# A hybrid encoder on one core: half of a shift vector summed on TensorE, small loads on another queue, the first loads reordered

## The chip, the core and the metric

The kernel runs on one core of a Trainium2 chip. The metric is the device time of one execution in microseconds (us). Engines are named as the profile names them: PE is TensorE (PEld its weight loads), DVE is VectorE, ACT is ScalarE, POOL is GpSimd, SP is SyncE, which issues nearly all DMA loads.

## The reference

Two layers work on 256 tokens of 1024 channels in fp32. Each layer is a feed-forward sub-layer (FFN), a token mixer (pooling in layer 0, latent attention in layer 1) and a second FFN. Every sub-layer is modulated by vectors that come from a condition `c`:

```python
sc = jax.nn.silu(c)
mod = (sc @ ada_w[i] + ada_b[i]).reshape(B, N_MOD, D_MODEL)[:, :, None, :]   # shift, scale, gate x 3

def modulated_sublayer(x, mod, g_pre, g_post, fn, weight):
    shift, scale, gate = mod[:, 0], mod[:, 1], mod[:, 2]
    h = rmsnorm(x, g_pre) * (1.0 + scale) + shift
    y = rmsnorm(fn(h), g_post)
    return x + weight * (1.0 + gate) * y

def swiglu(h, w_in, w_out):
    gate, up = jnp.split(h @ w_in, 2, axis=-1)
    return (jax.nn.silu(gate) * up) @ w_out
```

`sc` has 1024 entries and each layer's `ada_w` is 1024 x 9216, so a shift or a scale is a vector-matrix product of 1024 x 1024. The first FFN can't start before its shift and scale are known. The change touches only this opening.

## The kernel before

**Tiling.** The 256 tokens are two tiles of 128 (t = 0 and 1). A weight is loaded by SP in pieces of 128 x 2048 fp32 (1 MiB) into one of four raw buffers. It is then split for matmuls in a faster fp32 form: ACT casts it to a high part (`wi10H`, L263) and DVE subtracts to get a low part (`wi10L`, L271); a product is three matmuls (L98 to L100). The FFN goes through its 2816 columns in eleven chunks of 256. Pieces of the input weight are called by chunk and half of the 1024 rows: `wi10` is chunk 1, first half. Chunks 0 and 2 multiply their first half in plain fp32 (`task_in_whole`, matmuls at L794), without a split.

**Shift and scale.** A vector (m = 0 the shift, 1 the scale) is made in halves of 512 columns, each from two 1 MiB pieces (`adah`). DVE adds up eight terms, each a [128 x 512] weight times one column of `sc` (L350, then seven of L352), and PE sums over the partitions with the accumulated tile as weights and a column of ones as the moving operand (`ps_mod`, L361); DVE adds the bias (`mod`, L374). In this opening these are finished one after another as the code below calls them.

**The opening.** x is turned to [channel, token] tiles by PE (`ps_h`, L562, a half of 512 channels at a time), scaled and shifted into `hs` (ACT at L576 for one tile, DVE at L582 for the other), then split into `hTH` and `hTL`. `head_first` runs the first-half matmuls of chunks 0, 1 and 2 for both tiles, and between them steps a generator, `first_halves`, which brings in the second halves of shift and scale and the second halves of h; then the rest. Small matmuls on the identity (`warm`, L108) fill waits of PE.

**What sets the order.** Nothing is scheduled: each engine runs its instructions in the order in which the code issues them. Loads go out in the order of the list `first`, one list entry a task; a task's load is issued when one of the four raw buffers is free, that is, when DVE has finished the task four such pieces ahead (`Bulk.advance`). A DMA also takes one of eight completion lanes in turn, and waits until the lane's last DMA has landed.

Of the kernel before, what the change touches and what calls it, by code (L numbers as in the profile page):

```python
# [17 lines left out]
P = 128  # L18
D = 1024
# [20 lines left out]
def kernel(  # L40
# [71 lines left out]


    c_col = cpool.tile([P, KD], F32, name="c_col")
    nc.sync.dma_start(c_col, c_in.rearrange("o (p k) -> p (o k)", k=KD))
    xt = [rowp.tile([P, D], F32, tag=f"x{t}", name=f"x{t}", bufs=1) for t in range(NT)]

    def load_x(t):
        nc.sync.dma_start(xt[t], x_in[0, t * P : (t + 1) * P, :])
# [7 lines left out]
    ones = ones_r.bitcast(F32)  # L127
    mhalf = cpool.tile([P, 1], F32, name="mhalf")
    nc.vector.memset(mhalf, -0.5)
    sc = cpool.tile([P, KD], F32, name="sc")  # L130
    nc.scalar.activation(sc, c_col, AF.Silu)


    cols = cpool.tile([P, 96 + 144 + 3], F32, name="cols")
# [1 line left out]
    C_Q = 96 + 144  # L136
    C_KV = C_Q + 2

    def load_columns(parts, base):
        rows = rowp.tile([P, 512], F32, tag="bc", name="rows", bufs=4)[:, :P]  # L140
        n = 0
        for ap in parts:
            r = ap.shape[0]
            nc.sync.dma_start(rows[n : n + r, :], ap)
# [12 lines left out]
    def load_columns_late():  # L157
        return load_columns(
# [157 lines left out]
    def ada_half(layer, m, hf, accs, pieces=(1, 1)):  # L316

        st = {}
        wv = ada_w[layer].rearrange("(p k) n -> p k n", k=KD)
        c0 = m * D + hf * 512  # L320

        def load(q):
            def go():
                raw = raw_tile(f"adah{m}{hf}{q}")
                rv = raw.rearrange("p (k n) -> p k n", k=4)
                for k in range(0, 4, 4 // pieces[q]):
                    ks = slice(k, k + 4 // pieces[q])
# [1001 lines left out]


    accs = {}
    first = ada_half(0, 0, 0, accs) + ada_half(0, 1, 0, accs, (1, 2))
    with_load = lambda t, f: (t[0], lambda: (t[1](), f()), *t[2:])
    first[1] = with_load(first[1], lambda: load_x(0))
    first[2] = with_load(first[2], lambda: load_x(1))
    h01, h11 = ada_half(0, 0, 1, accs), ada_half(0, 1, 1, accs, (1, 2))
    first += [f0.task_in_whole(0, 0), h01[0], f0.task_in(1, 0), h01[1], *h11, f0.task_in_whole(2, 0)]
    ss1 = shift_scale(0, 1)
    first += [f0.task_in(0, 1), ss1[0], f0.task_in(1, 1), ss1[1], f0.task_in(2, 1), f0.task_out(0)]
    first += [ss1[2], f0.task_out(1), ss1[3], f0.task_in(3, 0), f0.task_in(3, 1)]  # L1340
# [50 lines left out]
        )  # L1391


    bulk.until(("adah", 0, 0, 1))
    turn_g()
    turn_b()
    bulk.finish_pe()
    s20 = first_rstd(0)
    xr0 = pre_xr(0, s20)
    bulk.until(("adah", 1, 0, 0))  # L1400
    bulk.finish()
    s21 = first_rstd(1)
    xr1 = pre_xr(1, s21)
    hT = [new_hT(0), new_hT(1)]
    turned = [turn_half(0, 0, xr0)]
    warm(6, "acc11", 1)
    turned += [turn_half(1, 0, xr1, psum.tile([P, 512], F32, tag="acc10", name="ps_h10", bufs=1))]
    warm(4, "acc11", 1)
    bulk.until(("adah", 1, 0, 1))
    bulk.finish()  # L1410
    parts = [mod_half(t, 0, ps, hT[t], 0, 0, t == 1) for t, ps in enumerate(turned)]

    def first_halves():
        bulk.until(("adah", 0, 1, 0))
# [12 lines left out]
        f0.high_in(0, 1)  # L1427
        bulk.finish()
        late += [turn_half(1, 1, xr1)]
        late = [mod_half(t, 1, ps, hT[t], 0, 0, t == 0) for t, ps in enumerate(late)]  # L1430
# [2 lines left out]
        for _, low, _ in late:  # L1433
            low()
        yield
        yield

    f0.head_first(hT, [p[2] for p in parts], first_halves())
    turn_late = load_columns_late()
    f0.unit(3, 0, hT[0])  # L1440
    f0.unit(3, 1, hT[1])
# [238 lines left out]
```

## Time and profile before

| | us |
|---|---|
| median of three runs (lowest, highest) | 925.95 (924.56, 929.2) |
| the profiled execution | 930.35 |
| its span | 928.6 |
| PE busy in the span | 898.9 |
| DVE busy | 703.9 |
| ACT busy | 437.3 |

The profiled execution is slower than the median by 4.4 us. The span leaves out 1.75 us around it. PE is busy 97% of the span; the forty slices of the page show the first one at 3 tenths for PE and all others but the last at 9. A busy PE need not be at full speed: the page's clock row is at 8 tenths in the second slice and in one near 645 us. The 16 DMA engines move 325 to 373 GB/s in four of the first five slices and 299 in the third.

### The profile page before, as it was taken

To read this page: it belongs to the slowest core of one execution; us is meant where nothing else is said; L and a number is where in the kernel's file an instruction comes from. 1 tells how busy PE (TensorE), PEld (TensorE's weight loads), DVE (VectorE), ACT (ScalarE), POOL (GpSimd) and SP (SyncE) were. 2 spreads that over 40 slices of the span, in tenths; PEclk is the share of its full clock that TensorE was granted. 3 is DMA by queue.
4 is the path that set the end of the run, shared out by engine and by line. 5 is a ranking of instruction groups with operands and counts; after the bars stand their busy time and mean duration, and the time that the engine had idled before them with its cause. 6 is when DMAs were issued, how large, how long until landed. Compare 5 with 4: busy or idle time off the path is not lost.

```text
span 928.6 us, 11171 instructions
## 1 busy us (share of the span) xinstructions
PE 898.9 (97%) x4251; PEld 733.0 (79%) x4251; DVE 703.9 (76%) x848; ACT 437.3 (47%) x653; POOL 41.8 (5%) x56
## 2 busy tenths in 40 slices
PE   3999999999999999999999999999999999999997
PEld 3568887887888888888888888888776888888885
DVE  5798888887877898797867987766798765656553
ACT  2255443345645434334742534337698654343421
POOL 0000000000000000000000000001163000000000
PEclk9899999999999999999999999998999999999999
DMA  9989998996357999898469999961143458857601
GB/s 325 368 299 343 360 373 313 351 359 242 137 180 264 378 339 326 297 387 275 137 183 360 324 351 327 344 229 59 46 137 113 160 153 280 293 193 259 227 1 45
DMA packets 135973, 235.28 MB, mean 253 GB/s; under 512 B 5628, under 2 KB 98415, under 8 KB 135664
## 3 DMA queue, kind: packets, MB, share of 16 engines
q1 hardware_dynamic: 135920, 234.58, 72.8%
q8 instruction: 33, 0.54, 0.2%
q14 instruction: 20, 0.16, 0.1%
HBM read 233.51 MB, written 1.05 MB: 253 GB/s over the span
## 4 chain that ended last, share of the span: by engine, by line
PE 88%; DVE 7%; issue 2%; DMA 1%; ACT 1%; POOL 0%; SPq 0%; DVEq 0%; POOLq 0%; ACTq 0%
PE acc L747 25%; PE in L100 16%; PE in L98 16%; PE in L99 16%; PE accm L1319 2%; PE ps_g L724 2%; DVE aacc L352 1%; PE ps_h L562 1%; PE ps_mod L361 1%; PE in L794 1%; DVE nm L1220 1%; DVE ql L1203 1%; DMA wo<-in_ffn_w_out_dram 1%; PE accp L965 1%; DMA adah<-in_ada_w_dram 1%
## 5 line engine op out<-in xcount | busy, mean ns | idle before, releaser
L352 DVE SCALAR_TENSOR_TENSOR aacc<-ada,sc,aacc 128x1024 f32<-128x1024 f32 (+1 forms) x113 | 143.8, 1272 | 9.9 <-DMA ada<-in_ada_w_dram 7.6
L708 ACT ACTIVATE sil<-in 128x256 f32<-128x256 f32 x84 | 32.2, 383 | 247.0 <-PE in L100 242.1
L710 DVE TENSOR_TENSOR g<-in,sil 128x256 f32<-128x256 f32 x84 | 35.2, 419 | 52.0 <-ACT sil L708 51.9
L95 DVE TENSOR_TENSOR gL<-ps_g,gH 128x256 fp32r<-128x256 f32 x88 | 36.6, 416 | 23.6 <-ACT gH L94 23.5
L94 ACT CAST gH<-ps_g 128x256 fp32r<-128x256 f32 x88 | 32.4, 368 | 44.5 <-PE ps_g L724 44.4
L503 POOL TENSOR_TENSOR r<-ms,mhalf 128x1 f32<-128x1 f32 x24 | 13.6, 565 | 840.5 <-DVE ms L501 840.5
L724 PEld LDWEIGHTS ps_g<-ident,g 128*128 128x128 f32 x176 | 24.7, 140 | 11.5
L724 PE MATMUL ps_g<-ident,g 128*128 128x128 f32 x176 | 33.6, 272 | 0.0
L508 ACT ACTIVATE junk<-x 128x512 bf16<-128x512 f32 x24 | 15.1, 631 | 21.1 <-DVE x L535 11.3
L361 PE MATMUL ps_mod<-ones,aacc 128*128 128x1 f32 x96 | 12.9, 262 | 10.9 <-DVE cols L150 9.7
L361 PEld LDWEIGHTS ps_mod<-ones,aacc 128*128 128x128 f32 x96 | 13.2, 213 | 11.9 <-DVE cols L150 10.0
L576 ACT ACTIVATE hs<-ps_h,mod,mod 128x128 f32<-128x128 f32 x48 | 18.0, 456 | 8.6 <-DVE mod L377 5.5
L352 DVE SCALAR_TENSOR_TENSOR aacc<-adah,sc,aacc 128x512 f32<-128x512 f32 x28 | 21.0, 751 | 0.9
L582 DVE TENSOR_SCALAR hs<-ps_h,mod,mod 128x128 f32<-128x128 f32 x48 | 16.4, 403 | 4.9 <-PE ps_h L562 4.6
L535 DVE SCALAR_TENSOR_TENSOR x<-tmp,r,x 128x512 f32<-128x512 f32 x23 | 16.3, 748 | 2.2 <-POOL r L503 1.2
L1238 POOL TENSOR_SCALAR p<-p,rs 128x256 f32<-128x256 f32 x16 | 16.1, 1008 | 26.8 <-ACT p L1228 16.4
L1228 ACT ACTIVATE p<-s,nm 128x256 f32<-128x256 f32 x32 | 15.0, 478 | 4.0 <-DVE nm L1220 2.6
L554 ACT ACTIVATE xr<-x,r 128x512 f32<-128x512 f32 x12 | 8.7, 722 | 17.4 <-POOL r L503 17.4
L593 DVE TENSOR_TENSOR hTL<-hs,hTH 128x512 fp32r<-128x512 f32 x24 | 15.6, 689 | 0.4
L271 DVE TENSOR_TENSOR wo10L<-wo,wo10H 128x2048 fp32r<-128x2048 f32 x4 | 9.2, 2292 | 8.1 <-ACT wo10H L263 8.1
L397 DVE TENSOR_REDUCE mod<-ps_turn 128x4 f32<-128x512 f32 x12 | 8.2, 687 | 8.1 <-PE ps_turn L391 8.1
L562 PE MATMUL ps_h<-ident,xr 128*128 128x128 f32 x96 | 13.7, 283 | 0.5 <-ACT xr L554 0.3
(498 smaller groups left out, 2880.3 us busy)
## 6 DMA issues: line engine op xcount, KB each, us to landing
wi<-in_ffn_w_in_dram SPq DMA_DIRECT2D x176, 512.0 KB, 5.8
ada<-in_ada_w_dram SPq DMA_DIRECT2D x64, 1024.0 KB, 7.1
wo<-in_ffn_w_out_dram SPq DMA_DIRECT2D x44, 1024.0 KB, 6.4
adah<-in_ada_w_dram SPq DMA_DIRECT2D x6, 1024.0 KB, 10.3
mwo<-in_mla_w_o_dram SPq DMA_DIRECT2D x4, 1024.0 KB, 6.1
bc<-in_ada_b_dram SPq DMA_DIRECT2D x12, 256.0 KB, 6.8
bc<-in_norm_g_dram SPq DMA_DIRECT2D x12, 256.0 KB, 7.4
adah<-in_ada_w_dram SPq DMA_DIRECT2D x4, 512.0 KB, 11.7
```

The lines of the kernel that those rows point to most:

```text
L94: nc.scalar.copy(h, src)
L95: nc.vector.tensor_sub(lo, src, h.bitcast(F32))
L98: nc.tensor.matmul(ps, lhsT=lh, rhs=rh, start=first, stop=False)
L99: nc.tensor.matmul(ps, lhsT=lh, rhs=rl, start=False, stop=False)
L100: nc.tensor.matmul(ps, lhsT=ll, rhs=rh, start=False, stop=last)
L352: nc.vector.scalar_tensor_tensor(acc, w, sc[:, k : k + 1], acc, op0=ALU.mult, op1=ALU.add)
L361: nc.tensor.matmul(ps[:, j : j + 1], lhsT=acc[:, (j - j0) * P : (j - j0 + 1) * P], rhs=ones[:, 0:1], start=True, stop=True,)
L562: nc.tensor.transpose(ps[:, j * P : (j + 1) * P], xr[:, kk * P : (kk + 1) * P], ident)
L708: nc.scalar.activation(sil, ps[:, 0:CW], AF.Silu)
L710: nc.vector.tensor_mul(g, ps[:, CW : 2 * CW], sil)
L724: nc.tensor.transpose(ps[:, a * P : (a + 1) * P], g[:, a * P : (a + 1) * P], ident)
L747: nc.tensor.matmul(acc[hf], lhsT=lhs[:, a, :], rhs=rhs[:, a, hf * 512 : (hf + 1) * 512], start=f, stop=l)
```

## The change

The first half of the first shift (layer 0, m = 0, columns 0 to 511) is summed on PE: `ada_half_pe` loads the two 1 MiB pieces in two DMAs each and runs 32 matmuls with a 128 x 128 block of the weight as the stationary operand and a column of `sc` as the moving one; a matmul with zeros opens the accumulation and one closes it. DVE adds only the bias (L390 of the new file). The loads of `c`, of the norm gains and of the biases are issued by ACT instead of SP. In `first`, wi00, wi10 and the second halves of shift and scale change places. xr0 is scaled by ACT alone, x of tile 1 is scaled and turned later, inside `first_halves`, and the ten small `warm` matmuls become four of 512 columns. The second half of the shift is reduced behind chunk 2's first group, that of the scale behind its second.

```diff
-    nc.sync.dma_start(c_col, c_in.rearrange("o (p k) -> p (o k)", k=KD))
+    nc.scalar.dma_start(c_col, c_in.rearrange("o (p k) -> p (o k)", k=KD))
...
+    zeros = cpool.tile([P, 4], F32, name="zeros")
+    nc.vector.memset(zeros, 0.0)
...
-    turn_g = load_columns([norm_g.rearrange("l m (j p) -> (l m j) p", p=P)], 0)
-    turn_b = load_columns([ada_b[0:1, :].rearrange("l (r p) -> (l r) p", p=P)], C_B)
+    turn_g = load_columns([norm_g.rearrange("l m (j p) -> (l m j) p", p=P)], 0, nc.scalar)
+    turn_b = load_columns([ada_b[0:1, :].rearrange("l (r p) -> (l r) p", p=P)], C_B, nc.scalar)
+
+    nc.scalar.activation(sc, c_col, AF.Silu)
...
+    def ada_half_pe(layer, m, pieces):
+        wv = ada_w[layer].rearrange("(p k) n -> p k n", k=KD)
+        c0 = m * D
+        st = {}
+
+        def load(q):
+            def go():
+                raw = raw_tile(f"adah{m}0{q}")
+                rv = raw.rearrange("p (k n) -> p k n", k=4)
+                for k in range(0, 4, 4 // pieces):
+                    ks = slice(k, k + 4 // pieces)
+                    nc.sync.dma_start(rv[:, ks, :], wv[:, 4 * q + ks.start : 4 * q + ks.stop, c0 : c0 + 512])
+                st[q] = rv
+
+            return go
+
+        def compute(q):
+            def go():
+                if q == 0:
+                    st["ps"] = tr_tile(f"ps_sum{m}")
+                    nc.tensor.matmul(st["ps"][:, 0:4], lhsT=ident, rhs=zeros, start=True, stop=False, skip_group_check=True)
+                ps, rv = st["ps"], st.pop(q)
+                for k in range(4):
+                    for j in range(4):
+                        nc.tensor.matmul(
+                            ps[:, j : j + 1],
+                            lhsT=rv[:, k, j * P : (j + 1) * P],
+                            rhs=sc[:, 4 * q + k : 4 * q + k + 1],
+                            start=False,
+                            stop=False,
+                            skip_group_check=True,
+                        )
+                if q == 1:
+                    nc.tensor.matmul(ps[:, 0:4], lhsT=ident, rhs=zeros, start=False, stop=True, skip_group_check=True)
...
+                    bulk.after.append(
+                        lambda: nc.vector.tensor_add(mods[layer, m][:, 0:4], ps[:, 0:4], cols[:, b : b + 4])
+                    )
...
-    first = ada_half(0, 0, 0, accs) + ada_half(0, 1, 0, accs, (1, 2))
+    first = ada_half_pe(0, 0, 2) + ada_half(0, 1, 0, accs, (2, 2))
...
-    first[2] = with_load(first[2], lambda: load_x(1))
+    first[3] = with_load(first[3], lambda: load_x(1))
...
-    first += [f0.task_in_whole(0, 0), h01[0], f0.task_in(1, 0), h01[1], *h11, f0.task_in_whole(2, 0)]
+    first += [f0.task_in_whole(0, 0), f0.task_in(1, 0), *h01, h11[0], f0.task_in_whole(2, 0), h11[1]]
...
     bulk.until(("adah", 1, 0, 0))
+    r0 = rstd(s20, 1.0)
     bulk.finish()
...
-    warm(6, "acc11", 1)
...
-    warm(4, "acc11", 1)
+    scratch = psum.tile([P, 512], F32, tag="acc11", name="warm", bufs=1)
+    for _ in range(4):
+        nc.tensor.matmul(scratch, lhsT=ident, rhs=xt[0][:, 0:512], start=True, stop=True)
     bulk.until(("adah", 1, 0, 1))
+    s21 = first_rstd(1)
     bulk.finish()
-    parts = [mod_half(t, 0, ps, hT[t], 0, 0, t == 1) for t, ps in enumerate(turned)]
+    parts = [mod_half(0, 0, turned[0], hT[0], 0, 0, False)]
+    h_first = [parts[0][2]]
+    xr1 = pre_xr(1, s21)
 
     def first_halves():
-        bulk.until(("adah", 0, 1, 0))
+        ps = turn_half(1, 0, xr1, psum.tile([P, 512], F32, tag="acc10", name="ps_h10", bufs=1))
+        parts.append(mod_half(1, 0, ps, hT[1], 0, 0, True))
+        h_first.append(parts[1][2])
         yield
         for high, low, _ in parts:
             high()
             low()
+        f0.high_in(1, 0)
         bulk.until(("wi", 0, 0, 1, 0))
+        bulk.until(("adah", 0, 1, 0))
         yield
         bulk.until(("adah", 0, 1, 1))
-        bulk.finish()
+        yield
+        bulk.until(("adah", 1, 1, 0))
+        yield
+        bulk.finish_pe()
         late = [turn_half(0, 1, xr0)]
-        yield
-        yield
         bulk.until(("adah", 1, 1, 1))
...
```

PE's queue before, from the first reduction (`ps_mod`) to the first FFN matmuls (`in`); `x4` counts instructions of the same kind in a row:

```order
L361 MATMUL ps_mod_134<-ones,aacc_111 128x1 x4
L562 MATMUL ps_h_176<-ident,xr_149 128x128 x4
L108 MATMUL warm<-ident 128x128 x6
L562 MATMUL ps_h_188<-ident,xr_169 128x128 x4
L108 MATMUL warm<-ident 128x128 x4
L361 MATMUL ps_mod_204<-ones,aacc_152 128x1 x4
L794 MATMUL in_222<-wi_116,hs_212 128x512 x4
L794 MATMUL in_234<-wi_116,hs_217 128x512 x4
```

The same place in the changed kernel, where `ps_sum` is the new sum:

```order
L373 MATMUL ps_sum_122<-zeros,ident 128x4
L377 MATMUL ps_sum_122<-sc,adah_108 128x1 x16
L377 MATMUL ps_sum_122<-sc,adah_111 128x1 x16
L386 MATMUL ps_sum_122<-zeros,ident 128x4
L611 MATMUL ps_h_190<-ident,xr_183 128x128 x4
L1457 MATMUL warm<-x_80,ident 128x512 x4
L410 MATMUL ps_mod_211<-ones,aacc_171 128x1 x4
L843 MATMUL in_231<-wi_140,hs_219 128x512 x4
L611 MATMUL ps_h_236<-ident,xr_228 128x128 x4
L843 MATMUL in_246<-wi_140,hs_241 128x512 x4
```

The sum and the wide `warm` group stand ahead of the scale's reduction (`ps_mod_211`), and tile 1's transposes (`ps_h_236`) now lie between the two tiles' matmuls of chunk 0.

DVE's queue before, from the shift's sum (`aacc_111`) to the scale's (`aacc_152`):

```order
L350 TENSOR_SCALAR aacc_111<-adah_100,sc 128x512
L352 SCALAR_TENSOR_TENSOR aacc_111<-adah_100,sc,aacc_111 128x512 x3
L352 SCALAR_TENSOR_TENSOR aacc_111<-adah_102,sc,aacc_111 128x512 x4
L150 COPY cols<-ps_cols 128x96
L150 COPY cols<-ps_cols 128x72
L501 SCALAR_TENSOR_TENSOR ms<-s_140 128x1
L555 TENSOR_SCALAR xr_149<-x_80,r 128x512
L350 TENSOR_SCALAR aacc_152<-adah_105,sc 128x512
L352 SCALAR_TENSOR_TENSOR aacc_152<-adah_105,sc,aacc_152 128x512 x3
L374 TENSOR_TENSOR mod_139<-ps_mod_134,cols 128x4
```

And in the changed kernel, from the scale's first half to h:

```order
L399 TENSOR_SCALAR aacc_171<-adah_115,sc 128x512
L401 SCALAR_TENSOR_TENSOR aacc_171<-adah_115,sc,aacc_171 128x512 x3
L550 SCALAR_TENSOR_TENSOR ms<-s_166 128x1
L390 TENSOR_TENSOR mod_163<-ps_sum_122,cols 128x4
L401 SCALAR_TENSOR_TENSOR aacc_171<-adah_118,sc,aacc_171 128x512 x4
L423 TENSOR_TENSOR mod_216<-ps_mod_211,cols 128x4
```

The shift's eight steps are gone from DVE; its bias add (`mod_163`), which reads PE's sum, stands ahead of the scale's last four steps.

PE's queue before, from chunk 2's first group (`first_0`) to the second half of chunk 0:

```order
L794 MATMUL first_0_296<-wi_247,hs_212 128x512 x4
L361 MATMUL ps_mod_317<-ones,aacc_152 128x1 x4
L562 MATMUL ps_h_324<-ident,xr_169 128x128 x4
L794 MATMUL first_1_297<-wi_247,hs_217 128x512 x4
L808 MATMUL in_222<-wi01H,hTH_172 128x512 x4
```

And in the changed kernel:

```order
L843 MATMUL first_0_312<-wi_259,hs_219 128x512 x4
L410 MATMUL ps_mod_318<-ones,aacc_265 128x1 x4
L611 MATMUL ps_h_323<-ident,xr_183 128x128 x4
L843 MATMUL first_1_313<-wi_259,hs_241 128x512 x4
L410 MATMUL ps_mod_340<-ones,aacc_171 128x1 x4
L611 MATMUL ps_h_348<-ident,xr_228 128x128 x4
L857 MATMUL in_231<-wi01H,hTH_186 128x512 x4
```

The scale's second reduction (`ps_mod_340`) comes behind chunk 2's second group now, next to the matmuls that need what is made from it.

## Rows read from the trace of the kernel before

**Rows 1.** Two stretches of PE: bounds, length, busy time (instructions), granted clock, DMA share, GB/s.

```profile
0.00:66.00 66.00, 49.11 (x194) 0.95 0.94 330
66.00:928.00 862.00, 849.82 (x4058) 0.99 0.72 248
```

**Rows 2.** Waits of PE from 60 us on: us in total, times, longest.

```profile
PE acc L747 <- DVE g L710: 1.1, 1, 1.1
```

**Rows 3.** Timeline: start, us, engine, line, operation, count, [idle before it, releaser].

```profile
2.11 0.94 SPq L328 DMA_DIRECT2D adah<-in_ada_w_dram  x2
...
7.44 0.48 DVE L350 TENSOR_SCALAR aacc<-adah,sc 128x512 f32<-128x512 f32 x1 [6.07 <-DMA adah<-in_ada_w_dram]
...
11.35 0.63 ACT L508 ACTIVATE junk<-x 128x512 bf16<-128x512 f32 x1 [8.64 <-DMA x<-in_x_dram]
...
13.65 1.78 PEld L361 LDWEIGHTS ps_mod<-ones,aacc 128*128 128x128 f32 x8 [9.99 <-DVE cols L150]
...
15.25 0.83 PEld L562 LDWEIGHTS ps_h<-ident,xr 128*128 128x128 f32 x4
...
16.06 2.68 PEld L108 LDWEIGHTS warm<-ident 128*128 128x128 f32 x12
...
19.30 0.53 PEld L562 LDWEIGHTS ps_h<-ident,xr 128*128 128x128 f32 x4 [0.55 <-ACT xr L554]
...
22.08 0.98 PEld L361 LDWEIGHTS ps_mod<-ones,aacc 128*128 128x128 f32 x8 [1.31 <-DVE aacc L352]
...
23.64 1.50 ACT L576 ACTIVATE hs<-ps_h,mod,mod 128x128 f32<-128x128 f32 x4 [4.39 <-DVE mod L377]
...
24.04 9.99 PE L794 MATMUL in<-wi,hs 128*128 128x512 f32 x16 [0.90 <-DVE hs L582]
...
25.02 0.63 ACT L590 CAST hTH<-hs 128x512 fp32r<-128x512 f32 x1
...
26.85 1.90 ACT L263 CAST wi10H<-wi 128x2048 fp32r<-128x2048 f32 x1 [1.21 <-DMA wi<-in_ffn_w_in_dram]
...
29.29 2.28 DVE L271 TENSOR_TENSOR wi10L<-wi,wi10H 128x2048 fp32r<-128x2048 f32 x1
...
37.70 0.47 DVE L350 TENSOR_SCALAR aacc<-adah,sc 128x512 f32<-128x512 f32 x1
...
38.21 5.48 DVE L352 SCALAR_TENSOR_TENSOR aacc<-adah,sc,aacc 128x512 f32<-128x512 f32 x7
...
40.66 3.59 PE L794 MATMUL first<-wi,hs 128*128 128x512 f32 x8
...
44.09 0.95 PE L361 MATMUL ps_mod<-ones,aacc 128*128 128x1 f32 x8
...
48.94 2.28 DVE L271 TENSOR_TENSOR wi01L<-wi,wi01H 128x2048 fp32r<-128x2048 f32 x1
```

**Rows 4.** Timeline of PE ahead of the attention layer, same columns.

```profile
640.70 1.84 PE L361 MATMUL ps_mod<-ones,aacc 128*128 128x1 f32 x16
642.40 1.07 PE L562 MATMUL ps_h<-ident,xr 128*128 128x128 f32 x8
643.31 2.58 PE L361 MATMUL ps_mod<-ones,aacc 128*128 128x1 f32 x16
```

**Rows 5.** Stretches of PE as in rows 1, where the granted clock falls.

```profile
23.00:24.00 1.00, 0.15 (x2) 0.50 1.09 358
...
644.00:644.50 0.50, 0.50 (x6) 0.72 0.00 0
644.50:645.00 0.50, 0.50 (x4) 0.50 0.00 0
```

**Rows 6.** All engines' busy time in a stretch; last: granted clock, DMA share, GB/s.

```profile
4.00:8.00 4.00, 0.00 (x0) 0.00 (x0) 0.53 (x2) 0.00 (x0) 0.00 (x0) 1.00 1.02 385
```

**Rows 7.** Timeline of PE's weight loads, chunk 0's first matmuls, columns as in rows 3.

```profile
28.47 0.34 PEld L794 LDWEIGHTS in<-wi,hs 128*128 128x128 f32 x1 [0.52 <-issue]
...
30.44 0.19 PEld L794 LDWEIGHTS in<-wi,hs 128*128 128x128 f32 x1 [0.24 <-issue]
```

More of the change, by code (lines that the diff above doesn't have):

```diff
@@ L137, with load_columns @@
     C_KV = C_Q + 2
-    def load_columns(parts, base):
+    def load_columns(parts, base, queue=nc.sync):
         rows = rowp.tile([P, 512], F32, tag="bc", name="rows", bufs=4)[:, :P]
@@ L143, in load_columns @@
             r = ap.shape[0]
-            nc.sync.dma_start(rows[n : n + r, :], ap)
+            queue.dma_start(rows[n : n + r, :], ap)
             n += r
@@ L346, in ada_half @@
         return [(("adah", m, hf, q), load(q), None, compute(q)) for q in range(2)]
+    def ada_half_pe(layer, m, pieces):
[29 more added lines that the diff above has]
+                    nc.tensor.matmul(ps[:, 0:4], lhsT=ident, rhs=zeros, start=False, stop=True, skip_group_check=True)
+                    mods[layer, m] = cpool.tile([P, KD], F32, name=f"mod{layer}{m}")
+                    b = C_B + layer * 72 + m * KD
+                    bulk.after.append(
+                        lambda: nc.vector.tensor_add(mods[layer, m][:, 0:4], ps[:, 0:4], cols[:, b : b + 4])
+                    )
+            return go
+        return [(("adah", m, 0, q), load(q), None, compute(q)) for q in range(2)]
     def ada_step(acc, w, k):
@@ L1391, in ffn_tail @@
         )
-    bulk.until(("adah", 0, 0, 1))
     turn_g()
     turn_b()
-    bulk.finish_pe()
+    bulk.until(("adah", 0, 0, 1))
     s20 = first_rstd(0)
-    xr0 = pre_xr(0, s20)
     bulk.until(("adah", 1, 0, 0))
+    r0 = rstd(s20, 1.0)
     bulk.finish()
-    s21 = first_rstd(1)
-    xr1 = pre_xr(1, s21)
+    xr0 = rowp.tile([P, D], F32, tag="xr", name="xr0")
+    for hf in range(2):
+        nc.scalar.activation(xr0[:, hf * 512 : (hf + 1) * 512], xt[0][:, hf * 512 : (hf + 1) * 512], AF.Copy, scale=r0)
     hT = [new_hT(0), new_hT(1)]
     turned = [turn_half(0, 0, xr0)]
-    warm(6, "acc11", 1)
-    turned += [turn_half(1, 0, xr1, psum.tile([P, 512], F32, tag="acc10", name="ps_h10", bufs=1))]
-    warm(4, "acc11", 1)
+    scratch = psum.tile([P, 512], F32, tag="acc11", name="warm", bufs=1)
+    for _ in range(4):
+        nc.tensor.matmul(scratch, lhsT=ident, rhs=xt[0][:, 0:512], start=True, stop=True)
     bulk.until(("adah", 1, 0, 1))
+    s21 = first_rstd(1)
     bulk.finish()
-    parts = [mod_half(t, 0, ps, hT[t], 0, 0, t == 1) for t, ps in enumerate(turned)]
+    parts = [mod_half(0, 0, turned[0], hT[0], 0, 0, False)]
+    h_first = [parts[0][2]]
+    xr1 = pre_xr(1, s21)
     def first_halves():
-        bulk.until(("adah", 0, 1, 0))
+        ps = turn_half(1, 0, xr1, psum.tile([P, 512], F32, tag="acc10", name="ps_h10", bufs=1))
+        parts.append(mod_half(1, 0, ps, hT[1], 0, 0, True))
+        h_first.append(parts[1][2])
         yield
@@ L1418, in first_halves @@
             low()
+        f0.high_in(1, 0)
         bulk.until(("wi", 0, 0, 1, 0))
+        bulk.until(("adah", 0, 1, 0))
         yield
         bulk.until(("adah", 0, 1, 1))
-        bulk.finish()
+        yield
+        bulk.until(("adah", 1, 1, 0))
+        yield
+        bulk.finish_pe()
         late = [turn_half(0, 1, xr0)]
-        yield
-        yield
         bulk.until(("adah", 1, 1, 1))
         f0.high_in(0, 1)
+        yield
         bulk.finish()
@@ L1435, in first_halves @@
         yield
-        yield
-    f0.head_first(hT, [p[2] for p in parts], first_halves())
+    f0.head_first(hT, h_first, first_halves())
     turn_late = load_columns_late()
```

1 line of the change is left out of this document (removed).

## The prediction

> **What bounds the kernel now.** I read the stretches first: TensorE (PE) is busy 849.8 of the 862 us behind 66 us, but 49.1 of the 66 us ahead of it [rows 1]. So from 66 us on only PE's own work counts, and the change, which lies wholly ahead of that point, can win or lose only by when PE gets there. What holds it there is the wait list: PE's last wait of the opening is 1.1 us for VectorE's g of the first feed-forward (FFN) layer [rows 2]. VectorE works in program order, so that wait goes back along its queue, over wo0L, wi11L and two sums, to wi01L, which ends at 48.94 + 2.28 = 51.2 us [rows 3]. The load that it needs as well, wo0, is issued only when VectorE frees a buffer two sums behind wi01L. From the end of wi01L on the order of every engine is the same in both kernels. **The time therefore moves by as much as the end of wi01L moves**, and I work out that one time for the changed kernel.
>
> **The sum on PE.** It takes one tensor_scalar and seven scalar_tensor_tensor from VectorE: 5.99 us by the same eight instructions at 37.70 [rows 3]. PE gets 32 matmuls of one column instead, with 128x128 fp32 weights each, and two with the zeros. The same form is there before: four program matmuls of ps_mod show as eight weight loads, 1.78 us at 13.65 and 0.98 us at 22.08 [rows 3], so 0.2225 us a pass at the low clock and 0.1225 at the full one. 34 matmuls are 68 passes: 15.1 us or 8.3 us. Which of the two is the question on which the forecast hangs.
>
> The clock column says 1.00 up to 23 us, but the pace says otherwise: at 13.65, after 10 us of idleness, the passes go at half the pace of 22.08 [rows 3]. The sum starts out of idleness too, so slow. Does it lift the clock? Ahead of the attention layer PE runs 16 passes of this one-column form, 8 transposes and 16 more, without a gap, from 640.70 [rows 4]; the granted clock falls there, to 0.72 over the slice from 644.0 and 0.50 in the next [rows 5]. An unbroken run of this form did not even hold the full level (2.4 GHz); I take it that it does not reach it from the low one (1.2 GHz) either.
>
> The Trainium skill ("TensorE: Matmul & The Clock Gate", section "Why this matters for your kernels") says the opposite for a run of matmuls in general: keep TensorE continuously busy and the full clock is granted. By that rule the sum would speed up on its way; the trace at 640 us disagrees for this form, and the measurement decides. It is the first rival below.
>
> **When it starts.** SP's first weight load is issued at 2.11 us, behind three small loads whose issue now lies on ScalarE's queue (ACT), so at 0.72 us, 1.39 earlier. It landed at 7.44 as the first sum began [rows 3]; it is cut in two now, and half a 1.05 MB piece is 1.36 us at 385 GB/s [rows 6]: 7.4 - 1.4 - 1.4 = 4.6 us. The sum runs from 4.7 to 4.7 + 15.1 = 19.8 us, the later pieces arriving faster than 16 passes take (3.6 us). If the small loads hold the first weights back by as much as they did before, it is 1.4 us more; that is one end for this step. The Trainium skill ("DMA: Bandwidth & Descriptors", section "Issuing engines are not separate DMA queues") says that loads of several issuing engines interleave on the same 16 DMA engines and only issue time is saved. By it the start would lie between these two; no run here has loads from ACT.
>
> **What waits for it.** On VectorE the add that makes the shift (mod_163) stands ahead of the second half of the scale's sum, four steps, and waits for PE. So those steps, whose last data come eight such pieces behind the first, at 4.6 + 8 x 1.36 = 15.5 us, run from 19.9 to 20.1 + 4 x 0.78 = 23.2 us (0.78 from 5.48 / 7) [rows 3]; before, they ended at 22.1. On PE the four transposes of xr0 follow (0.83 us at the low clock [rows 3]): 20.7. Then come four dense matmuls of 512 columns, eight passes of 0.86 us low or 0.43 full, by the spacing (a weight load and the gap before it: 0.34 + 0.52 at 28.47, 0.19 + 0.24 at 30.44) [rows 7]. When the clock rises in them I bound by two cases: dense passes began at 16.06 and by 19.30 the pace was full (3.2 us); they began at 24.04, the spacing was still 0.86 at 28.47 and 0.43 at 30.44; half way is 29.4, 5.4 us [rows 3, 7]. That gives 25.7 and 26.8 us for the end; I take the middle, 26.25. Only then comes ps_mod of the scale, though its data are there at 23.2. From ps_mod to the first FFN matmul it was 22.09 to 24.04; 1.95 us [rows 3]. **First FFN matmul: 28.2 us, against 24.04.**
>
> **From there to wi01L.** The first four matmuls of token tile 0 take 3.4 us at the full clock (8 passes, 40.66 to 44.09 [rows 3]): 31.6. The transposes of tile 1 come only now (0.53 plus some 0.1 to release ACT): 32.2. ACT then has hs (1.50), the cast hTH (0.63) and wi10H (1.90) in this order, though wi10's data are there at 15.5 + 5 x 1.36 = 22.3: 36.3; VectorE's wi10L 2.28: 38.6, against 31.57 [rows 3]. PE ends its own first chunk at 36.1 and waits 2.5 us for it. Then 24 passes of chunk 1, ps_mod and four transposes, which took from 34.03 to 40.66 before (24.04 + 9.99 to 40.66 [rows 3]), less the one pass that needs no wi10L: 6.4; and two groups of chunk 2, 3.43 each: 38.6 + 6.4 + 6.9 = 51.9 us. VectorE's 16 sum steps take 2 x 5.99 from 38.6 and end at 50.6, just inside. Then the chain from the last ps_mod (44.09) to the end of wi01L (51.2), 7.1 us [rows 3]: **59.0 us, 7.8 later than 51.2.** Part of it is the lost cover: the second group of chunk 2 (3.4 us) stood beside this chain, and now stands ahead of the ps_mod that starts it.
>
> What I cost at nothing: zeros' memset and the split of xr0 (ACT does both halves, 0.7 us beside PE's sum); the other first loads, hidden as PE and VectorE are the late ones; if the sum were quick, the scale's last piece would be what counts (second rival). The profiled execution is 930.35 us, so 938.15 by its own measure; it lies 4.4 above the median of the three runs, 925.95, and the shift does not depend on that: 925.95 + 7.8 = 933.8.
>
> **Rivals.**
> (1) The clock rises in the sum. For it: nothing here shows a long sum of this form out of idleness, and dense passes did it in 3.2 us. Against it: [rows 4, 5]. If it rose at 4.7 + 3.2 = 7.9, 14 passes were slow and 54 take 6.6: 14.5. Then xr0 is late: x0 lands at 4.6 + 4 x 1.36 = 10.0, its square sums, 0.74 each from 11.35 [rows 3], are ready early, but rstd's first step stands behind the first half of the scale's sum on VectorE, which ends at 12.8 + 1.6 = 14.4; some 0.8 for rstd and as much for xr0 make it 15.9; transposes 0.5, dense passes 3.4: 19.8, first FFN matmul 21.8. Behind it the same 30.8 us (28.2 to 59.0): 52.6, 1.4 us later, 927.4. It decides as soon as the sum ends before 15.9; a rise halfway, at about 12 us, gives some 3 us, 929. This is the case that is not slower: within half a per cent.
> (2) The loads decide alone: the scale's last piece at 15.5, two steps 1.6, ps_mod to the first matmul 1.95: 19.0. Then 19.0 + 30.8 = 49.8, 1.4 us sooner, 924.5. For it: VectorE is 6 us lighter. Against it: the dense group alone ends later even at the full clock. This is as early as it can be, so a gain of over half a per cent needs my 30.8 us to be 3 us too long as well.
> (3) The clock falls again between the dense group and the first FFN matmul, as it had before at 23 us [rows 5], with the eight one-column passes of 22.08 as its only work since the second dense group. Then eight passes cost 3.4 us more: 59.0 + 3.4, 937.2. The pause is 1.95 us here, a bit shorter.
>
> **Chances.** Forecast 0.62, own range 932 to 936 (the two rise times, the late start, 1.5 us of slack in the chain). Rival 3: 0.13. Rival 1 with its halfway form: 0.21. Rival 2 and anything better: 0.04. Half a per cent, 4.6 us, is about what a measurement can tell from no change: forecast and rival 3 lie beyond it, all but a rest of 0.01 of the forecast, slower 0.74; rivals 1 and 2 within it, same 0.23; faster 0.03 for an error of both kinds in rival 2. The range from 927 to 937.5 leaves out rival 2 and the dear half of rival 3.
>
> **What would show it.** The sum's 64 one-column passes spaced 0.22 us and ending near 20 (right), or 0.12 us and near 14.5 (rival 1). The dense group ending near 26, spaced 0.86 at first. The first FFN matmul at 28, wi10L ending near 39 with PE waiting for it, wi01L ending near 59. If wi01L ends late but PE behind 66 us is not shifted by as much, my claim that this one time carries through is wrong; if the first FFN matmul is at 28 and wi01L before 55, my 30.8 us is.

## The result, and the profile after

The changed kernel takes 941.2 us (median of 4, 937.2 to 943.0) against 925.3 us for the kernel before in the same measurement (median of 4, 924.3 to 929.2): 15.9 us more by these medians. The measured ratio is 1.0134 (95% interval 1.0101 to 1.0167), or 12.4 us. It is smaller than the quotient of the two medians, 1.017, and fits the experiments below, where the kernel before had a median of 928.5 to 928.8 us in each of three groups. The changed kernel is slower, as forecast, but by 12.4 us or more instead of 7.8, and 941.2 lies outside the range of 927 to 937.5. The profiled execution took 943.0 us, with a span of 941.1.

First the opening on PE. This is the timeline of the kernel after, with the columns of [rows 3]; the rows answer to those of ps_mod, ps_h, the warm matmuls and L794 there.

```profile
5.07 0.40 PE L150 MATMUL ps_cols<-ident,rows 96*128 96x96 f32 x1 [5.07 <-DMA rows<-in_norm_g_dram]
6.54 0.38 PE L150 MATMUL ps_cols<-ident,rows 72*128 72x72 f32 x1 [1.08 <-DMA rows<-in_ada_b_dram]
6.72 0.52 PE L373 MATMUL ps_sum<-zeros,ident 128*128 128x4 f32 x2
7.10 13.79 PE L377 MATMUL ps_sum<-sc,adah 128*128 128x1 f32 x64
...
21.18 1.09 PE L611 MATMUL ps_h<-ident,xr 128*128 128x128 f32 x4
22.06 5.09 PE L1457 MATMUL warm<-x,ident 128*128 128x512 f32 x8
26.99 0.95 PE L410 MATMUL ps_mod<-ones,aacc 128*128 128x1 f32 x8
28.84 3.70 PE L843 MATMUL in<-wi,hs 128*128 128x512 f32 x8 [0.90 <-DVE hs L631]
...
39.20 0.50 PE L99 MATMUL first<-wi10L,hTH 128*128 128x512 f32 x1 [1.74 <-DVE wi10L L274]
...
52.71 0.95 PE L410 MATMUL ps_mod<-ones,aacc 128*128 128x1 f32 x8
```

The 64 passes of the sum run unbroken from 7.1 to 20.9 us, 0.2155 us each. That is the pace of the low clock in [rows 3], and no pass of the 64 is quicker: from start to start each takes 0.212 to 0.215 us. The sum begins at 7.1 because the two transposes of the norm gains and biases stand ahead of it on PE, and their rows arrive only at 5.07 and 6.54 us now.

VectorE over the same stretch, of the kernel after:

```profile
21.36 0.16 DVE L390 TENSOR_TENSOR mod<-ps_sum,cols 128x4 f32<-128x4 f32 x1 [6.54 <-PE ps_sum L386]
21.45 3.12 DVE L401 SCALAR_TENSOR_TENSOR aacc<-adah,sc,aacc 128x512 f32<-128x512 f32 x4
...
36.85 2.29 DVE L274 TENSOR_TENSOR wi10L<-wi,wi10H 128x2048 fp32r<-128x2048 f32 x1
...
57.55 2.29 DVE L274 TENSOR_TENSOR wi01L<-wi,wi01H 128x2048 fp32r<-128x2048 f32 x1
```

The bias add waits 6.54 us for the sum on PE, and the last four steps of the scale's sum, whose data are long there, wait behind it. wi01L ends at 57.55 + 2.29 = 59.84 us, against 51.22 in [rows 3].

The waits of PE between 0 and 66 us (us in total, times, longest), where [rows 2] stood before:

```profile
PE ps_cols L150 <- DMA rows<-in_norm_g_dram: 5.1, 1, 5.1
PE in L857 <- DVE hTH L637: 1.8, 1, 1.8
PE first L99 <- DVE wi10L L274: 1.7, 1, 1.7
PE ps_cols L150 <- DMA rows<-in_ada_b_dram: 1.1, 1, 1.1
PE in L843 <- DVE hs L631: 0.9, 1, 0.9
```

PE's waits after the sum add up to about 5 us. So the loss is not waiting alone; PE also has its own slow passes, in the sum and in the first of the wide matmuls (0.85 us from start to start, 0.43 at the end of the group).

The stretches of [rows 1], of the kernel after, with PE's busy time first behind the width:

```profile
0.00:66.00 66.00, 54.45 (x207) 39.41 (x208) 36.19 (x62) 17.60 (x29) 1.79 (x8) 0.97 0.81 280
66.00:941.00 875.00, 861.77 (x4093) 707.78 (x4091) 662.35 (x779) 420.61 (x626) 39.85 (x48) 0.99 0.71 248
```

PE is busier in the first 66 us (54.5 against 49.1), yet behind 66 us it is busy for 12 us more (861.8 against 849.8): work that the kernel before had done by then, and some more.

### The profile page after: what moved, and what is told of

Read it like the earlier page. It is cut to its first block, busy times and chain, and to the rows that moved or that the text cites. A ratio compares the mean times of both kernels' runs of the same rounds, so it can differ in the third digit from the quotient of the medians.

```text
span 941.1 us, 11266 instructions
## 1 busy us (share of the span) xinstructions
PE 916.2 (97%) x4299; PEld 747.2 (79%) x4299; DVE 698.5 (74%) x840; ACT 438.2 (47%) x654; POOL 41.6 (4%) x56
## 4 chain that ended last, share of the span: by engine, by line
PE 89%; DVE 6%; issue 2%; ACT 1%; DMA 1%; POOL 0%; ACTq 0%; DVEq 0%; POOLq 0%
PE acc L796 25%; PE in L100 16%; PE in L98 16%; PE in L99 16%; PE accm L1368 2%; PE ps_g L773 2%; PE ps_sum L377 1%; PE ps_h L611 1%; PE ps_mod L410 1%; PE accp L1014 1%; DVE nm L1269 1%; DVE ql L1252 1%; DMA wo<-in_ffn_w_out_dram 1%; PE first L843 1%; PE ps_turn L440 1%
## 5 line engine op out<-in xcount | busy, mean ns | idle before, releaser
L94 ACT CAST gH<-ps_g 128x256 fp32r<-128x256 f32 x88 | 32.4, 368 | 44.0 <-PE ps_g L773 44.0
L557 ACT ACTIVATE junk<-x 128x512 bf16<-128x512 f32 x24 | 15.1, 631 | 19.2 <-DVE x L584 11.2
L625 ACT ACTIVATE hs<-ps_h,mod,mod 128x128 f32<-128x128 f32 x48 | 18.0, 456 | 12.4 <-PE ps_h L611 7.9
L401 DVE SCALAR_TENSOR_TENSOR aacc<-adah,sc,aacc 128x512 f32<-128x512 f32 x21 | 15.8, 752 | 0.8
L611 PEld LDWEIGHTS ps_h<-ident,xr 128*128 128x128 f32 x96 | 12.6, 157 | 2.0 <-issue 0.7
L377 PE MATMUL ps_sum<-sc,adah 128*128 128x1 f32 x64 | 13.8, 352 | 0.0
```

What stands on the lines that cost most here:

```text
L94: nc.scalar.copy(h, src)
L377: nc.tensor.matmul(ps[:, j : j + 1], lhsT=rv[:, k, j * P : (j + 1) * P], rhs=sc[:, 4 * q + k : 4 * q + k + 1], start=False, stop=False, sk ...
L401: nc.vector.scalar_tensor_tensor(acc, w, sc[:, k : k + 1], acc, op0=ALU.mult, op1=ALU.add)
L611: nc.tensor.transpose(ps[:, j * P : (j + 1) * P], xr[:, kk * P : (kk + 1) * P], ident)
```

## The experiments

Each kernel ran beside the kernel before on the same chip, in three groups; that kernel's median there was 928.5, 928.7 and 928.8 us. "The end of wi01L" is the time on which the prediction rests, and "the first FFN matmul" is the start of L794 and the lines that answer to it.

**The kernel before and the changed kernel, again.** No edit.

> The kernel before, unchanged, to learn how much executions of one and the same kernel differ and where. Theory A (the 12 us of the profile are 8 us of the opening, as forecast, and some 4 us of clock falls in the pooling stage that happen to differ): ratio 1.000, times between 924 and 930, and in this trace the end of wi01L lies at 51.2 us again within 0.3 us. Rival B (the profiled execution of before was a slow one in the opening too, since the clock had fallen at 23 us just ahead of the first FFN matmuls): ratio 1.000 too, but in a faster execution the clock stays at 1.00 there, the sixteen passes of chunk 0 take 7 us instead of 10, and wi01L ends 2 us sooner, near 49.0 us; the opening then costs the changed kernel 10 us rather than 8.

> The changed kernel, unchanged. Theory A: 937 to 943 us, ratio 1.010 to 1.017 again; the one-column sum ends at 21 us and wi01L at 59.8 us within 0.5 us, as both hang on the low clock in the sum; what differs between executions is the clock in the pooling stage (220 to 270 us), between no fall (3 us less than in the first trace of this kernel, 0 to 5 us of offset gained there) and two falls. Rival C (the shift of 8 us itself sets the pooling stage's clock, in every execution): two additional falls there again, at 240 and 260 us.

Measured: 928.45 us (ratio 0.9998, 0.9986 to 1.001) and 941.01 us (1.013, 1.0107 to 1.0154). Timeline of the kernel before in this second profile, PE and then VectorE:

```profile
23.94 8.63 PE L794 MATMUL in<-wi,hs 128*128 128x512 f32 x16 [0.90 <-DVE hs L582]
...
42.63 0.95 PE L361 MATMUL ps_mod<-ones,aacc 128*128 128x1 f32 x8
...
62.70 0.48 PE L747 MATMUL acc<-wo0H,gH 128*128 128x512 f32 x1
...
29.18 2.29 DVE L271 TENSOR_TENSOR wi10L<-wi,wi10H 128x2048 fp32r<-128x2048 f32 x1
...
47.47 2.29 DVE L271 TENSOR_TENSOR wi01L<-wi,wi01H 128x2048 fp32r<-128x2048 f32 x1
```

And of the changed kernel in its second profile:

```profile
29.40 3.70 PE L843 MATMUL in<-wi,hs 128*128 128x512 f32 x8 [0.90 <-DVE hs L631]
...
73.39 0.48 PE L796 MATMUL acc<-wo0H,gH 128*128 128x512 f32 x1
...
58.12 2.29 DVE L274 TENSOR_TENSOR wi01L<-wi,wi01H 128x2048 fp32r<-128x2048 f32 x1
```

Chunk 0's sixteen passes in the kernel before took 8.63 us here and 9.99 in [rows 3]. The granted clock over the next stretch says why; this is the first profile of before, and then this one (width, PE busy, granted clock, DMA share, GB/s):

```profile
28.00:31.00 3.00, 3.00 (x6) 0.70 1.05 390
```

```profile
28.00:31.00 3.00, 3.00 (x8) 1.00 1.05 388
```

The clock fell at 23 us in both, but came back sooner here. wi01L ends at 49.76 us, 1.46 sooner than in the profile from which I forecast, in an execution of 928.51 us, which is the median. So rival B holds in part: 1.5 us instead of its 2, with the clock low for a shorter time and not at 1.00 throughout. Theory A had 51.2. Executions of the kernel before go with their mean granted clock: 924.4 us at 0.999, 928.5 at 0.992, 931.3 at 0.988. The changed kernel's second profile (941.01 us, its median) has wi01L's end at 58.12 + 2.29 = 60.41, so between these two executions the opening costs 60.41 - 49.76 = 10.65 us. The first wo0 matmul comes 13.0 us behind that end in both profiles of both kernels (12.94 to 12.99), so up to there the delay is handed on whole. In the pooling stage the clock of this second profile fell once, at 258 us; rival C, two more falls in every execution, is out.

**Only the sum on PE.** The kernel before with `ada_half_pe` for the first half of the shift:

```diff
-    first = ada_half(0, 0, 0, accs) + ada_half(0, 1, 0, accs, (1, 2))
+    first = ada_half_pe(0, 0, 1) + ada_half(0, 1, 0, accs, (1, 2))
```

> The kernel before with one part of the change alone: the first half of the first shift summed on TensorE, in whole pieces; order of the loads, queues and small matmuls as before. Theory (the sum runs at the low clock and the scale's sum on VectorE waits behind its bias add): sum from 7.4 us, 68 passes of 0.22 us, to 22.5 us; the scale's last four steps end near 27 us instead of 22; first FFN matmul near 29.6 us instead of 24.0; wi01L ends 4 to 6 us later than before; 930 to 932 us. Rival (the loss is in the new order, not in the sum): wi01L within 1 us of 51.2 and the time within 1 us of before.

Measured: 938.82 us, ratio 1.0113 (1.0084 to 1.0141). PE and then VectorE of this kernel:

```profile
7.44 13.78 PE L376 MATMUL ps_sum<-sc,adah 128*128 128x1 f32 x64 [5.35 <-DMA adah<-in_ada_w_dram]
21.09 0.57 PE L385 MATMUL ps_sum<-zeros,ident 128*128 128x4 f32 x2
21.51 0.40 PE L151 MATMUL ps_cols<-ident,rows 96*128 96x96 f32 x1
...
33.21 7.13 PE L842 MATMUL in<-wi,hs 128*128 128x512 f32 x16 [0.90 <-DVE hs L630]
...
22.68 0.23 DVE L152 COPY cols<-ps_cols 128x72 f32<-128x72 f32 x1 [0.48 <-PE ps_cols L151]
...
24.05 0.48 DVE L398 TENSOR_SCALAR aacc<-adah,sc 128x512 f32<-128x512 f32 x1
...
56.30 2.28 DVE L273 TENSOR_TENSOR wi01L<-wi,wi01H 128x2048 fp32r<-128x2048 f32 x1
```

At 938.8 instead of 930 to 932 us it lost more than I expected: the transposes of the small rows stand behind the sum on PE, VectorE's copies wait for them, and so the scale's whole sum starts at 24.05 us instead of 14.78. The first FFN matmul is at 33.21. But from there to the end of wi01L it is 58.58 - 33.21 = 25.4 us, against 25.8 in the kernel before: the old order loses nothing behind the first FFN matmul.

**The sum back on VectorE.** The changed kernel with all else kept:

```diff
-    first = ada_half_pe(0, 0, 2) + ada_half(0, 1, 0, accs, (2, 2))
+    first = ada_half(0, 0, 0, accs, (2, 2)) + ada_half(0, 1, 0, accs, (2, 2))
...
     bulk.until(("adah", 0, 0, 1))
+    bulk.finish_pe()
```

The added line issues the shift's reduction on PE as soon as VectorE's sum is done.

> The changed kernel with the sum put back on VectorE; loads on ScalarE's queue, order of loads, one wide group of dense matmuls and the new order of the halves are kept. Theory: the scale's sum ends at 18 us instead of 24.6, but the dense group starts only when xr0 is there (16.2 us) and ends at 22 to 24 us; first FFN matmul at 24 to 26 us against 28.8 in the changed kernel; wi01L 31 us behind that, 55 to 57 us, so 3 to 5 us faster than the changed kernel and still 4 to 6 us slower than before: 929 to 932 us. Rival (all of the loss is the sum): as fast as before or faster, 923 to 926 us.

Measured: 939.26 us, ratio 1.0113 (1.0092 to 1.0134). PE and VectorE of this kernel:

```profile
25.53 3.70 PE L843 MATMUL in<-wi,hs 128*128 128x512 f32 x8 [0.90 <-DVE hs L631]
...
54.25 2.28 DVE L274 TENSOR_TENSOR wi01L<-wi,wi01H 128x2048 fp32r<-128x2048 f32 x1
```

The first FFN matmul comes 3.3 us sooner than in the first profile of the changed kernel, and wi01L ends at 56.53, again 31.0 us behind it. That is still 6.8 us later than in the median profile of the kernel before. So most of the loss stays when the sum leaves PE. The opening came out as I expected, the time did not: 939.3 instead of 929 to 932 us. It is 10.7 us more than before, of which the opening explains 6.8. Some 1.1 of the other 4 us is the drift of the added tile (below). In this profile the granted clock also fell three times between 237 and 261 us; what such stretches cost on average is open.

**The sum with dense matmuls in between.** Twenty warm matmuls ahead of the sum, two of 128 columns behind every four of one column, and two wide ones instead of four:

```diff
+                    st["dense"] = psum.tile([P, 512], F32, tag="acc11", name="dense", bufs=1)
...
+                    for _ in range(2):
+                        nc.tensor.matmul(st["dense"][:, 0:P], lhsT=ident, rhs=ident, start=True, stop=True)
...
+    warm(20, "acc10", 1)
     turn_g()
...
-    for _ in range(4):
+    for _ in range(2):
```

> The changed kernel with 20 small warm matmuls ahead of the sum, two matmuls of 128 columns behind every four one-column ones, and two dense 512-column matmuls instead of four: the sum should run at the full clock, 0.11 us a pass instead of 0.2155. Theory 1 (the slow pace of the sum holds the first FFN matmul back): the sum ends at 17 to 19 us instead of 20.9, the first FFN matmul comes at 23 to 25 instead of 28.8 to 29.4, wi01L ends at 54 to 56 instead of 59.8, time 935 to 937. Rival (the new order of the opening loses most by itself, from the first FFN matmul on): wi01L still ends 31 us behind the first FFN matmul, so at best 54, against 49.8 in an ordinary execution of before; the time stays 6 or more above 928.5. If the sum isn't what holds, the first FFN matmul stays at 28 to 29 and the time at 940 to 941.

Measured: 943.5 us, ratio 1.0154 (1.0127 to 1.0181), not faster than the changed kernel itself (941.0 us; the two intervals overlap). PE of this kernel, and under it the granted clock (behind the width and PE's busy time):

```profile
8.43 1.03 PE L378 MATMUL ps_sum<-sc,adah 128*128 128x1 f32 x8
...
13.26 1.71 PE L378 MATMUL ps_sum<-sc,adah 128*128 128x1 f32 x8
...
31.74 3.70 PE L846 MATMUL in<-wi,hs 128*128 128x512 f32 x8 [0.90 <-DVE hs L634]
```

```profile
11.00:12.00 1.00, 1.00 (x11) 0.86 1.04 385
12.00:14.00 2.00, 2.00 (x11) 0.50 1.04 385
14.00:20.00 6.00, 6.00 (x30) 0.50 1.07 367
```

The sum did start at the full clock: eight passes in 1.03 us. But the granted clock fell to 0.50 between 11 and 12 us, in the middle of unbroken work with 128-column matmuls in it, and stayed there until the wide matmuls; the sum ended at 26.5 us instead of the 17 to 19 expected. So in this run the sum did not keep the clock up even when it had it. What a sum wholly at the full clock would bring was therefore not tested. wi01L ends 62.71 - 31.74 = 31.0 us behind the first FFN matmul once more.

**Without the wide matmuls.** The four matmuls of 512 columns taken out of the changed kernel:

```diff
-    scratch = psum.tile([P, 512], F32, tag="acc11", name="warm", bufs=1)
-    for _ in range(4):
-        nc.tensor.matmul(scratch, lhsT=ident, rhs=xt[0][:, 0:512], start=True, stop=True)
```

> The changed kernel without the four matmuls of 512 columns. They stand between the sum and ps_mod and took 4.9 us. Theory: ps_mod comes at 24.6 instead of 27.0 and the first FFN matmul at 26.5, but chunk 0's eight passes then go at the low clock (6.9 us instead of 3.7), so wi01L ends at 58 to 60 as before, time 939 to 942. Rival (the dense group is pure loss): wi01L at 57.5, time 938.5.

Measured: 941.26 us, ratio 1.0134 (1.011 to 1.0157), the same as the changed kernel. PE and VectorE:

```profile
24.69 1.84 PE L410 MATMUL ps_mod<-ones,aacc 128*128 128x1 f32 x8 [2.43 <-DVE aacc L401]
27.43 5.15 PE L843 MATMUL in<-wi,hs 128*128 128x512 f32 x8 [0.90 <-DVE hs L631]
...
74.66 1.05 PE L796 MATMUL acc<-wo0H,gH 128*128 128x512 f32 x2
...
57.58 2.28 DVE L274 TENSOR_TENSOR wi01L<-wi,wi01H 128x2048 fp32r<-128x2048 f32 x1
```

As the theory had it: ps_mod comes 2.3 us sooner, but at the low pace (1.84 instead of 0.95 us), and the first FFN passes take 5.15 us instead of 3.70. wi01L ends at 59.86. The first wo0 matmul is 14.8 us behind that here, not 13.0: the granted clock was 0.50 from 58 to 64 us, while in the changed kernel's second profile it was back at 1.00 from 61 us on.

**A later start in the old order.** The kernel before with 24 idle VectorE steps ahead of the first sum:

```diff
+    idle = rowp.tile([P, 512], F32, tag="bc", name="idle", bufs=4)
+    nc.vector.memset(idle, 0.0)
+    for _ in range(24):
+        nc.vector.scalar_tensor_tensor(idle, idle, mhalf, idle, op0=ALU.mult, op1=ALU.add)
     bulk.until(("adah", 0, 0, 1))
```

> The kernel before with 24 idle VectorE steps of 0.78 us ahead of the first sum, nothing else: the opening starts some 10 us later, in the old order. Theory 1 (the rest of the program is only shifted): the first wo0 matmul comes at 71.5 to 73 instead of 62.7, and the time is 928.5 plus the same 9 to 10 us: 937.5 to 938.5. Rival (a later opening brings the clock down more often behind it, in the pooling stage, whatever made it late): time 940 to 942, with more low-clock stretches between 227 and 275 us than the kernel before has.

Measured: 941.29 us, ratio 1.0139 (1.0115 to 1.0162). VectorE:

```profile
61.05 2.29 DVE L271 TENSOR_TENSOR wi01L<-wi,wi01H 128x2048 fp32r<-128x2048 f32 x1
```

wi01L ends at 61.05 + 2.29 = 63.34, so the shift came out as 13.6 us and not 10. The profiled execution is 941.81 us: 13.3 more than the profiled 928.51 of before. A shift in the opening therefore carries through nearly one to one here, and being late did not by itself cost anything behind it. The rival's mechanism did not show: the granted clock fell once between 227 and 275 us, against twice in the second profile of before. Its number of 940 to 942 was met only because the shift was larger than meant.

**One more tile.** In the kernels with the line below PE drifted later behind 66 us, against the kernel before; in the two without it at that time it had not.

```diff
+    zeros = cpool.tile([P, 4], F32, name="zeros")
+    nc.vector.memset(zeros, 0.0)
```

> The kernel before with one more tile, zeros (128x4) and its memset, which nothing reads. In the six runs with this tile (the changed kernel and its variants, the PE sum alone) the PE instructions behind 66 us drift later by some 0.25 us per 200 us against the kernel before, 0.8 to 1 us by the end; the two without it (late_start, act_queue) show no drift. Theory (the tile, by moving the addresses of what follows, makes the drift): the offset to the kernel before grows by 0.8 to 1 us between 66 and 900 us, time 929 to 930 against 928.5. Rival (the drift belongs to the changed opening or to the PE sum): offset constant, time 928.5.

Measured: 930.97 us, ratio 1.0021 (1.0004 to 1.0038). The same two PE instructions of the kernel before (second profile) and of this one:

```profile
267.06 0.48 PE L747 MATMUL acc<-wo0H,gH 128*128 128x512 f32 x1
...
629.80 0.62 PE L747 MATMUL acc<-wo9H,gL 128*128 128x512 f32 x2
```

```profile
270.19 0.48 PE L749 MATMUL acc<-wo0H,gH 128*128 128x512 f32 x1
...
633.48 0.62 PE L749 MATMUL acc<-wo9H,gL 128*128 128x512 f32 x2
```

The offset grows from 3.13 to 3.68 us between these two, a stretch in which the clock falls in neither kernel. Over the same stretch it grows by 0.55 to 0.57 us in all seven profiles of kernels with the tile, this one among them, and by 0.01 at most in the four kernels without it and in the first profile of before. With the stretches from 66 to 187 us (0.2) and from 733 to 915 us (0.3) the steady drift is some 1.1 us. The theory holds for that: a tile that nothing reads, with its memset, brings the drift, and the changed kernel carries it. The rest of this profile's offset is not the tile's alone: 0.7 us of it arises between 187 and 199 us, where PE waits shortly for VectorE, and the third version under "Only the loads", without the tile, loses 0.5 us there as well. What in the tile does it (it moves the addresses of all later tiles) is not shown.

**Only the loads.** The kernel before with the small loads on ACT's queue and the scale's first half in two pieces each; in a second version x of tile 1 keeps its old place, and a third adds four warm matmuls behind the second ps_mod. The edit of the first, beside the two of the change's diff for the queue:

```diff
-    first = ada_half(0, 0, 0, accs) + ada_half(0, 1, 0, accs, (1, 2))
+    first = ada_half(0, 0, 0, accs, (2, 2)) + ada_half(0, 1, 0, accs, (2, 2))
...
-    first[2] = with_load(first[2], lambda: load_x(1))
+    first[3] = with_load(first[3], lambda: load_x(1))
```

> The kernel before with only the loads changed: the three small loads on ACT's queue and the first half of the scale in two pieces each. Sum on VectorE and order of the code as before. Theory (the order of the opening and the sum are what costs, the loads are not): the second sum ends at 18.7 to 19.5 us instead of 22.1, the first FFN matmul comes at 20.5 to 21.5 instead of 23.9, wi01L ends at 46.5 to 49 against 49.8, time 924.5 to 927.5 against 928.5. Rival (the later loads bound the opening, not the sums): wi01L stays at 49 to 50, time 928 to 929. If the loads on ACT's queue hold the rest up, the first FFN matmul is later than 23.9 and the time above 929.

> act_queue with x of tile 1 loaded one piece earlier again, as in the kernel before. In act_queue VectorE waited 2.65 us at 16 us for the square sums of this tile. Theory: the wait goes, the scale's sum ends at 19.5 to 20.5 us instead of 22.9, the first FFN matmul comes at 21.5 to 22.5 instead of 25.7 (23.9 in the kernel before), wi01L ends at 47.5 to 49.5, time 926 to 928 against 928.5. Rival (the later loads bound it, or the clock falls longer in an earlier opening): first FFN matmul 22 but wi01L at 49.5 to 51 and the time at 928.5 to 930.

> The same with four warm matmuls (128 columns) behind the second ps_mod, in PE's pause of 0.9 us ahead of the first FFN matmul. Theory (the clock falls there because of the pause): no or a shorter low-clock stretch at the first FFN matmul, 1.7 us or more sooner than without, time 924.5 to 926.5. Rival (the one-column matmuls ahead bring it down, the pause does not matter): same low-clock stretch, same time as without, within 1 us.

Measured: 932.4 us (ratio 1.0039, 1.002 to 1.0057), 926.92 us (0.9974, 0.9959 to 0.9989) and 926.38 us (0.9971, 0.9961 to 0.9982). VectorE of the first version, then of the second:

```profile
18.57 0.16 DVE L502 SCALAR_TENSOR_TENSOR ms<-s 128x1 f32<-128x1 f32 x1 [2.65 <-ACT junk L509]
...
50.51 2.29 DVE L272 TENSOR_TENSOR wi01L<-wi,wi01H 128x2048 fp32r<-128x2048 f32 x1
```

```profile
4.93 0.49 DVE L351 TENSOR_SCALAR aacc<-adah,sc 128x512 f32<-128x512 f32 x1 [3.56 <-DMA adah<-in_ada_w_dram]
...
45.77 2.28 DVE L272 TENSOR_TENSOR wi01L<-wi,wi01H 128x2048 fp32r<-128x2048 f32 x1
```

In the first, x of tile 1 came too late for the old order: VectorE waits 2.65 us for its square sums with the scale's last four steps behind it, and my expectation of a gain was wrong. With x in its place the first sum starts at 4.93 us instead of 7.34 and the first FFN matmul comes at 22.41 instead of 23.94; 926.9 us is the expected time, and 0.26% less than the kernel before. The profile of this version is of one of its fast executions (923.03 us), so its rows show the order of events better than the gain. The warm matmuls bring nothing beyond that which a measurement can tell; in the profiles of the second and third version the clock did not fall at the first FFN matmul at all, so their theory was not put to the test. The second and third version are faster than the kernel before by a small margin that is clear of the noise, and they hold only the load part of the change.

## Why the prediction was right in direction and wrong in size

**The sum on PE: right.** The forecast had the low pace for all passes and an end at 19.8 us; it was 0.2155 us a pass and 20.9, and in the sum with dense matmuls in between even a start at the full clock was lost. Rival 1 is refuted. The Trainium skill ("TensorE: Matmul & The Clock Gate", section "Why this matters for your kernels") has TensorE kept busy without a break reach the full clock; 13.8 us of unbroken one-column passes did not get there in this trace. The start was mis-sized: I had 4.7 us, with 1.4 more at one end, and missed that the transposes of the small rows stand ahead of the sum on PE and that their rows, on ACT's queue, are there only at 5.07 and 6.54 instead of some 3.3 us. The weights were in time, as forecast: VectorE starts on them at 4.93 us in the second version under "Only the loads". The later start is 2.4 us, of which 1.1 remained at the sum's end, as the passes were cheaper than I had them.

**The first FFN matmul: nearly right.** 28.84 and 29.40 us in two profiles against 28.2. ps_mod followed the wide matmuls at 26.99 and 27.56 (forecast 26.25).

**From there to wi01L: right.** 30.8 us forecast, 31.0 in both profiles of the changed kernel, with the sum on VectorE and with the warmed sum (32.4 without the wide matmuls, where the first passes are slow). Its parts, in the second profiles of the two kernels: from the first FFN matmul to the end of wi10L 10.3 us instead of 7.5, as tile 1's transposes and hs come later; from there to the last ps_mod 13.6 instead of 11.2, as chunk 2's second group now stands ahead of it (no run moved this group alone); the rest 7.13 in both. So of the 10.65 us, 5.2 come from this order and 5.5 from the later first FFN matmul. Taking the sum off PE leaves 6.8 of them.

**The base: this is the step that failed.** "it lies 4.4 above the median of the three runs, 925.95, and the shift does not depend on that". It did. The profiled execution was slow partly in the opening itself, where the clock stayed low until some 30 us [rows 7]; I took its wi01L end of 51.2 as the mark, and added the shift to a median of executions that need not have that stretch in full. In the one profile of a median execution the mark is 49.76. And the median of three runs was itself low, by luck of which executions they were: over 55 executions beside the experiments it is 928.5 to 928.8.

The 7.2 us between the forecast (933.8) and the median of the changed kernel's nine runs (941.0) come out as: 2.6 for the base, 928.5 instead of 925.95; 1.46 for the mark; 1.4 for wi01L at 60.41 instead of 59.0, 1.2 of it in the first FFN matmul; and 1.8 behind the opening (from the first wo0 matmul to the end it is 867.6 us against 865.8 in the two second profiles). With base and mark put right the forecast would have been some 937.8, just beyond the range as well: the two smaller terms count too.

**"PE behind 66 us is only shifted": nearly.** In the late start a shift cost nothing more. But the changed kernel has 1.8 us more there. 0.5 of it lies outside the profiled span, which leaves out 2.3 us of the execution's time instead of 1.8. About 1.1 is the steady drift that the added tile brings. Low-clock stretches in the pooling and attention stages add and take away more than the rest, and differ from one execution to the next of either kernel: the first profile of the changed kernel fell to the low clock three times between 240 and 264 us, the second once. How many a kernel has on average stays open.

**Rival 3** took place in another form: the clock fell not ahead of the first FFN matmul but at 55 us, where PE waits 1.8 us for hTH. In the two profiles of the changed kernel that cost nothing on the path: PE still reached the matmuls on wi01L as wi01L ended, and the first wo0 matmul stayed 13.0 us behind it. Without the wide matmuls the stretch lasted longer and cost 1.8 us. **Rival 2** did not happen: the loads alone, in the old order, do give its kind of gain (926.9 us), but the change ties them to the sum on PE and to the new order.

## What to carry to other kernels

A shift read from one profile must be added to that profile's own time, or better, both must be read in a profile whose time is the median of many executions: 4 of the 7 us of error were there. Before moving a reduction to TensorE as one-column matmuls, price it at the low clock (here 13.8 us against 6.0 on VectorE) and list what stands behind it on both engines. And keep what covers a chain beside that chain: the stretch up to the ps_mod that starts the chain grew by 2.4 us with one more group of matmuls (3.4 us) in it, more than the loads alone won (1.9 us).

## What the runs showed of the hardware

- A run of one-column fp32 matmuls with 128 x 128 weights neither reached the full clock (64 passes at 0.2155 us in the changed kernel) nor held it: in the warmed sum the granted clock fell from 1.00 to 0.50 between 11 and 12 us, in unbroken work, though two 128-column matmuls stood behind every four of them.
- Small loads on ACT's queue, issued beside large ones on SP's, could be used by PE at 5.07 and 6.54 us in the first profile of the changed kernel (4.83 to 6.07 for the first of them in the other profiles in which PE waits for them); on SP's queue, ahead of the large ones, at 3.30 to 3.41 us in the kernel before.
- A 128 x 4 tile that nothing reads, with its memset, made PE drift later by some 1.1 us over the program. The time with it was 0.2% longer (0.04 to 0.38%).
